# Hard-max attention on one core: last four tiles compared whole in fp32, first flag segment as words, key units of the second batch three tiles later

## The chip, the cores and the metric

One core of one Trainium2 chip runs the kernel. The metric is the device time of one execution in microseconds (us), the median of several runs. Every run also has a span, from the first to the last instruction in its trace, about 2 us shorter than the time. Unless said otherwise, times inside a run are us from the start of that span.

A **ratio** below is the mean time of one kernel's fast runs over that of the kernel before in the same rounds, so it is not quite the ratio of the medians that are quoted. Its 95% interval stands in brackets.

## The reference, cut to what matters

```python
B, Sq, Sk, D = 4, 4096, 4096, 128          # float32
logits = np.matmul(q, k.transpose(0, 2, 1))
best = np.argmax(logits, axis=-1)
return v[b_idx, best, :].astype(np.float32)
```

For each query the kernel must find the key with the largest dot product and copy that key's value row.

## The kernel before

There are 128 query tiles of 128 queries, 32 per batch. For each tile TensorE forms scores, ScalarE (ACT) and VectorE (DVE) fold groups of four keys into one packed word, and a MAX8 keeps the best eight groups. GpSimd (POOL) then **gathers** the keys of the best group (kg), VectorE forms fp16 dot products of three key differences and picks the winner, GpSimd gathers the value rows (vr), and SyncE (SP) stores them. Every gather is one GpSimd transfer of 128 rows.

Queries for which the screen is too close to call are **flagged**. They are compacted in two segments (tiles 0 to 63 during the run, tiles 64 to 127 at the end), their keys (FK) and query (FQ) are gathered in fp32 and compared exactly, the winner's value row (FV) is gathered, and a last GpSimd transfer **scatters** these rows over the output. A fallback for too many flagged rows lies behind a branch that is skipped here.

The first segment fetched the record of a flagged query (FR) before it could fetch its keys:

```python
def flag_segment(t0, t1, ready, stored):
    ...                                      # one-hot product gives tile and row: tp, rw, row, rr
    get(FR, rec, rr, P * T)                  # gather of the record
    get(FQ, q_flat, row, P * T)
    yield "until", lambda: not fast, 3
    ...                                      # bo, gi, gb from FR on VectorE
    for r in range(3):
        get(FK[:, r, :], k_flat, gb[:, r:r + 1], B * Sk)
    yield "until", lambda: not fast, 3
    win = yield from exact(FK, FQ, gb, 3, f"f{t0}")      # 12 fp32 dots on VectorE
    get(FV, v_flat, win, B * Sk)
    ...
```

The end of the kernel, where late(n) issues value gathers that are due:

```python
def flags_last(t0, t1, ready, fill, late):
    ...
    late(LATE)
    get(FK[:, 0, :], k_flat, gb[:, 0:1], B * Sk)
    get(FQ, q_flat, row, P * T)
    for r in (1, 2):
        get(FK[:, r, :], k_flat, gb[:, r:r + 1], B * Sk)
    yield                                    # whole tiles are compared here
    ...
    late(1 << 20)                            # the rest of the value gathers, then their stores
    ...
    win = whole(ex)
    all_rows(hi)                             # the skipped fallback: every engine jumps
    get(FV, v_flat, win, B * Sk)
    nc.gpsimd.indirect_dma_start(out=out_flat, out_offset=IOA(ap=rowk, axis=0), in_=FV, in_offset=None, ...)   # the scatter
```

The last two tiles are compared whole: all four keys of the best group are gathered in fp32 (xk), dotted, and picked. Key units (unit_k) prepare the next batch's keys, one ACT copy each:

```python
for b in range(1, B):
    x = b * NQT
    units += [(x - 1, x - NQT + (6 + 3 * i // 2 if b == 1 else 1 + 2 * i), unit_k, b, i) for i in range(16)]
```

## Time and profile before

| | kernel before |
|---|---|
| time, median of 3 | 438.59 us (438.47 to 438.96) |
| VectorE, ScalarE, GpSimd busy | 93%, 87%, 70% |
| last gather that waits for VectorE | 397.23 us |
| last value gather, scatter | 426.44, 432.35 us |

The page's second part shows, for 40 equal slices of the span, each engine's busy share in tenths:

```profile
DVE  2788999999999999999999999999999999999961
ACT  4999999999999999999999888999999988985010
POOL 8423456777767786777778776777767677777773
```

VectorE stays at 9 nearly to the end; GpSimd shows 7, but a gather is recorded with 1.0 us and followed by 0.3 in which GpSimd is not counted busy, so a 7 to 8 is a full GpSimd. The chain of what ended last goes on behind the two steps that the prediction shows. Columns are start, length, and what:

```profile
431.57 0.56 issue
432.12 1.25 POOLq L927
```

From the end of the scatter's last wait (431.57), 0.56 pass until GpSimd's sequencer goes on behind the scatter. The scatter itself is recorded 0.23 later, at 432.35, so **0.79 after its last wait**.

### The profile page before, as it was taken

What the parts mean: (1) busy time and instruction counts of PE and PEld (TensorE: products, weight loads), DVE (VectorE), ACT (ScalarE), POOL (GpSimd) and SP (SyncE); (2) the same over time, 40 slices, a digit from 0 to 9 for tenths busy, and PEclk for the clock granted to TensorE, in tenths of its full rate; (3) what the DMA queues carried; (4) which work ended last, traced back from release to release, by engine and by line L of the source; (5) the groups of instructions that cost most, each with busy time, mean ns of one, the idle gap of its engine ahead of it and who ended that gap; (6) DMA issues with size and microseconds to landing.
All of it is one profiled execution on the core that took longest, in us unless ns stands there. A gap on an engine that the chain in (4) does not pass through costs nothing.

```text
span 436.5 us, 6165 instructions
## 1 busy us (share of the span) xinstructions
PE 377.1 (86%) x1830; PEld 167.7 (38%) x1830; DVE 406.6 (93%) x722; ACT 378.2 (87%) x446; POOL 304.3 (70%) x335
## 2 busy tenths in 40 slices
PE   7999999999999999999999888989889988885010
PEld 4444444444444444444444433433333333332000
DVE  2788999999999999999999999999999999999961
ACT  4999999999999999999999888999999988985010
POOL 8423456777767786777778776777767677777773
PEclk9999999999999999999999999999999999999555
DMA  7943999473326999663336985452423232333441
GB/s 127 204 108 72 158 141 144 103 134 81 108 55 133 174 166 189 127 113 100 92 95 138 172 148 116 93 143 76 119 76 92 82 85 81 93 95 99 116 131 52
DMA packets 52868, 50.54 MB, mean 116 GB/s; under 512 B 34136, under 2 KB 40890, under 8 KB 52832
## 3 DMA queue, kind: packets, MB, share of 16 engines
q0 software_dynamic: 19072, 33.87, 39.7%
q1 hardware_dynamic: 33760, 16.26, 15.8%
q8 instruction: 14, 0.23, 0.2%
q14 instruction: 22, 0.18, 0.2%
HBM read 40.05 MB, written 14.55 MB: 125 GB/s over the span
## 4 chain that ended last, share of the span: by engine, by line
ACT 37%; issue 23%; DVE 16%; PE 9%; POOL 8%; DMA 6%; POOLq 0%; ACTq 0%; DVEq 0%; SPq 0%
ACT A L245 32%; DVE TOP L275 6%; ACT E L258 5%; DVE W L271 5%; POOL vr L353 4%; PE psn L228 3%; POOL kg L293 3%; PE pd L228 3%; PE psn L255 3%; DMA vr<-in_v_dram,win 2%; DMA natk<-in_k_dram 2%; DVE prod L311 1%; DVE p L316 1%; DMA vr<-in_v_dram,win_w 1%; DMA kg<-k,cand 1%
## 5 line engine op out<-in xcount | busy, mean ns | idle before, releaser
L245 ACT ACTIVATE A<-pd 128x1024 f16<-128x1024 f32 x253 | 257.0, 1043 | 10.8 <-PE pd L228 10.3
L293 POOL DMA_INDIRECT kg<-k,cand x126 | 124.5, 988 | 79.8 <-DVE cand L287 48.8
L271 DVE SCALAR_TENSOR_TENSOR W<-psn,E 128x1024 int16<-128x1024 f32 x128 | 166.4, 1300 | 6.8 <-PE psn L255 4.1
L228 PE MATMUL psn<-kT,qT 128*128 128x512 f16 x512 | 151.9, 378 | 16.2 <-ACT A L245 7.5
L228 PE MATMUL pd<-kT,qT 128*128 128x512 f16 x506 | 150.4, 379 | 6.6 <-ACT A L245 6.3
L275 DVE MAX8 TOP<-W 128x8 f32<-128x1024 f32 x128 | 156.0, 1219 | 0.0
L228 PEld LDWEIGHTS <-qT 128*128 128x128 f16 x1018 | 97.2, 97 | 153.0 <-issue 62.9
L353 POOL DMA_INDIRECT vr<-in_v_dram,win x126 | 125.9, 1000 | 39.5 <-issue 35.3
L255 PE MATMUL psn<-A,identh 128*128 128x512 f16 x512 | 152.0, 378 | 0.0
L258 ACT ACTIVATE E<-psn 128x1024 int16<-128x1024 f32 x128 | 132.3, 1033 | 4.6 <-PE psn L255 4.1
L255 PEld LDWEIGHTS <-identh 128*128 128x128 f16 x512 | 49.6, 97 | 60.8
L311 DVE TENSOR_TENSOR prod<-kg,natq 128x768 f16<-128x768 f16 x63 | 34.4, 546 | 0.2 <-DMA kg<-k,cand 0.2
L208 ACT ACTIVATE kT<-uk 128x256 f16<-128x256 f32 x48 | 20.4, 426 | 0.8 <-PE uk L205 0.8
L316 DVE TENSOR_TENSOR p<-prod 128x768 f16<-128x768 f16 (+1 forms) x34 | 17.7, 520 | 0.2
L321 DVE TENSOR_REDUCE D<-p 128x12 f32<-128x384 f16 (+1 forms) x34 | 17.2, 506 | 0.1
L204 PE MATMUL uk<-identh,natk 128*128 128x128 f16 x96 | 15.8, 218 | 0.0
L512 ACT ACTIVATE far_e<-iota_h,posn_e 128x128 f16<-128x128 f16 x2 | 0.8, 393 | 14.7 <-DVE posn_e L504 14.7
L495 PE MATMUL fp_e<-n_e,tri 128*128 128x1 f32 x2 | 0.6, 348 | 13.9 <-DVE n_e L493 13.9
L205 PEld LDWEIGHTS <-natk 128*128 128x128 f16 x96 | 9.3, 97 | 7.0 <-issue 4.5
L66 POOL DMA_DIRECT2D natk<-in_k_dram x19 | 11.3, 601 | 0.8 <-POOLq L916 0.8
L204 PEld LDWEIGHTS <-natk 128*128 128x128 f16 x96 | 9.4, 98 | 5.6
L319 DVE TENSOR_TENSOR p<-p 128x384 f16<-128x384 f16 (+1 forms) x34 | 11.3, 331 | 0.1
(158 smaller groups left out, 153.4 us busy)
## 6 DMA issues: line engine op xcount, KB each, us to landing
out_dram<-vr SPq DMA_DIRECT2D x31, 256.0 KB, 2.2
natq<-in_q_dram POOLq DMA_DIRECT2D x12, 256.0 KB, 5.3
natk<-in_k_dram POOLq DMA_DIRECT2D x10, 256.0 KB, 5.7
k<-kd SPq DMA_DIRECT2D x18, 128.0 KB, 3.4
k<-natk POOLq DMA_DIRECT2D x6, 384.0 KB
kg<-k,cand POOLq DMA_INDIRECT x126, 2.7
vr<-in_v_dram,win POOLq DMA_INDIRECT x126, 2.7
natk<-in_k_dram POOLq DMA_DIRECT2D x8, 128.0 KB, 6.5
```

What stands on the lines that cost most here:

```text
L204: nc.tensor.matmul(out=o, lhsT=natk[b % 2][:, h, 4 * m + x, :], rhs=identh, start=True, stop=False)
L208: nc.scalar.activation(out=kT[b % 2][:, c:c + 256], in_=ps, func=AF.Copy)
L228: nc.tensor.matmul(out=ps[:, n * 512:(n + 1) * 512], lhsT=qT[b % 2][:, qt * P:(qt + 1) * P], rhs=kT[b % 2][:, u * 1024 + n * 512:u * 1024 ...
L245: nc.scalar.activation(out=A, in_=ps, func=AF.Abs)
L255: nc.tensor.matmul(out=ps[:, n * 512:(n + 1) * 512], lhsT=identh, rhs=A[:, n * 512:(n + 1) * 512], start=False, stop=True)
L258: nc.scalar.activation(out=E, in_=ps, func=AF.Relu, scale=QSCALE)
L271: nc.vector.scalar_tensor_tensor(out=W_t[t % NW].bitcast(I16)[:, 1::2], in0=ps, scalar=QSCALE, in1=E, op0=OP.mult, op1=OP.max)
L275: nc.vector.max(out=TOP[:, t, :], in_=W_t[t % NW].bitcast(FP32))
L293: near_q.append(lambda j=j: nc.gpsimd.indirect_dma_start(out=kg[:, j].rearrange("p f d -> p (f d)"), out_offset=None, in_=k16[t0 // NQT], ...
L311: nc.vector.tensor_tensor(out=prod[:, i:i + h], in0=kg[:, i:i + h], in1=natq[b % 2][:, x + i - b * NQT:x + i + h - b * NQT, :].unsqueeze(2 ...
L316: nc.vector.tensor_tensor(out=p1, in0=prod[:, :, :, 0:64], in1=prod[:, :, :, 64:128], op=OP.add)
L353: late_q.append(lambda j=j: nc.gpsimd.indirect_dma_start(out=vr[:, j, :], out_offset=None, in_=v_flat, in_offset=IOA(ap=win[:, i + j:i + j ...
```

## The change

The intent was to bring the flag work of the end forward (four whole tiles behind the flag gathers, and no pick for them ahead), to save the gather FR by carrying the group words through the one-hot product, and to fill ScalarE's early tiles more evenly. Its core, cut:

```diff
-LATE = 4
+LATE = 2
+WHOLE = 4
@@ flag_segment
+        low_words(t0, S)                      # words of the three best groups
+        EC = ...; nc.vector.tensor_tensor(out=EC, in0=CG, in1=F..., op=OP.mult)
+        nc.vector.max(out=e8[:, r], in_=EC[:, r])         # r = 0..3
+        for i, x in enumerate((F, F4)):       # counts, on ScalarE now
+            nc.scalar.activation(out=junk, in_=x, func=AF.Copy, accum_out=n3[:, i:i + 1])
...
-            nc.tensor.matmul(out=ps2[:, 0:2], lhsT=OH[:, s, :], rhs=rec2[:, s, :], ...)
+            nc.tensor.matmul(out=ps2[:, 0:6], lhsT=OH[:, s, :], rhs=rec6[:, s, :], ...)
+        gb, row = places(t0, ps2)
-        get(FR, rec, rr, P * T)
         get(FQ, q_flat, row, P * T)
-        yield "until", lambda: not fast, 3
-        (bo, gi, gb from FR)
@@ pick_whole
-        put_values(len(chunks) - 1, 0, 2, win, ...)
+        for i in range(0, WHOLE, 2):
+            put_values(len(chunks) - 1, i, i + 2, win, ...)
@@ tiles per chunk
-    cuts = ... + [T - 2, T]
+    cuts = ... + [T - 6, T - 4, T]
@@ key units
-        (6 + 3 * i // 2 if b == 1 else 1 + 2 * i)
+        (9 + 3 * i // 2 if b == 1 else 1 + 2 * i)
@@ end of the program
-    drain one pick; last_picks inside flags_last; dots_whole(0); dots_whole(1)
+    drain(left("dots")); drain(left("pick")); late_now(2)
+    for i in range(WHOLE):
+        dots_whole(i)
```

Below, the three parts are called the **early shift**, the **words** and the **whole tiles**.

## The prediction

> **What bounds the kernel now.** I read the windows table by stage first, then the timelines of ScalarE (ACT) and VectorE (DVE) side by side, and last the chain that ended last with the GpSimd (POOL) timeline of the tail. Times are us from the span's start. Tiles are the 128 query tiles; a tile costs ACT two A (L245) and one E (L258), and DVE one fold W (L271), one MAX8 (L275) and a share of the fp16 dot products.
>
> ```profile
> 20.00:50.00 30.00, 28.82 (x148) 13.22 (x146) 26.37 (x27) 30.00 (x38) 11.64 (x13) 1.00 0.59 109
> 50.00:100.00 50.00, 48.68 (x247) 22.23 (x246) 49.66 (x71) 50.00 (x63) 31.19 (x33) 1.00 0.81 133
> 250.00:300.00 50.00, 45.79 (x225) 20.24 (x224) 49.90 (x88) 46.68 (x56) 37.33 (x38) 1.00 0.56 119
> 410.00:437.00 27.00, 1.95 (x10) 1.52 (x10) 13.43 (x90) 1.31 (x4) 15.56 (x15) 0.50 0.37 106
> ```
>
> Columns after the length: PE, PEld, DVE, ACT, POOL busy. From 20 to 50 ACT is full (30.00 of 30) and DVE has 3.6 us free. From 50 to about 225 both are full. From there to 397 only DVE is (49.90 of 50 against ACT's 46.68). After 410 nobody is full: this stage is a chain.
>
> The early stage, ACT and then DVE:
>
> ```profile
> 28.32 1.02 ACT L258 ACTIVATE E<-psn 128x1024 int16<-128x1024 f32 x1
> 30.14 0.39 ACT L208 ACTIVATE kT<-uk 128x256 f16<-128x256 f32 x1
> 101.46 1.12 ACT L258 ACTIVATE E<-psn 128x1024 int16<-128x1024 f32 x1
> ```
>
> ```profile
> 29.68 1.31 DVE L271 SCALAR_TENSOR_TENSOR W<-psn,E 128x1024 int16<-128x1024 f32 x1 [0.75 <-PE psn L255]
> 103.65 1.29 DVE L271 SCALAR_TENSOR_TENSOR W<-psn,E 128x1024 int16<-128x1024 f32 x1
> ```
>
> The lag from the start of a tile's E to the start of its fold is 1.36 where DVE waits (29.68 - 28.32), and I find 1.35 to 1.36 as the usual floor of waiting folds once key units run. It is 103.65 - 101.46 = 2.19 at tile 30, with no wait: there DVE is behind by its own work. The kT copy of a key unit (L208) costs ACT some 0.35 (two tiles with one take 3.08 and 3.05, those without 2.71).
>
> The tail, by POOL:
>
> ```profile
> 397.23 0.96 POOL L293 DMA_INDIRECT kg<-k,cand  x1 [0.47 <-DVE cand L287]
> 410.26 1.37 POOL L353 DMA_INDIRECT vr<-in_v_dram,win  x1 [0.30 <-issue]
> 418.51 1.01 POOL L528 DMA_INDIRECT FK<-in_k_dram,gb_e  x1 [0.30 <-DVE XD L585]
> 426.44 1.02 POOL L353 DMA_INDIRECT vr<-in_v_dram,win_w  x1 [0.30 <-issue]
> 428.30 1.00 POOL L528 DMA_INDIRECT FV<-in_v_dram,xw_fe  x1 [0.84 <-DVE xw_fe L623]
> 432.35 1.02 POOL L557 DMA_INDIRECT out_dram<-FV,rowk_e  x1 [3.05 <-DMA out_dram<-vr]
> ```
>
> and by the chain of what released what:
>
> ```profile
> 426.44 2.75 DMA vr<-in_v_dram,win_w
> 429.27 2.09 DMA out_dram<-vr
> ```
>
> The gather at 397.23 is the last one that had to wait for DVE. Behind it POOL issues 22 gathers, up to the one at 426.44, with 0.3 between each two: 29.21 / 22 = 1.33 each, and no wait. The last of them (values of the last tiles) lands, its store lands at 431.36, and only then may the scatter of the flagged rows go. The other branch, flag keys FK to winner to FV (428.30), is ready some 0.4 before the store (428.30 + 2.7 = 431.0, an estimate from the 2.7 that the page gives as the median landing of such gathers). So the end is set by the **number of POOL gathers behind 397.23**, and DVE's flag work is close behind but not on the path.
>
> **What the Trainium skill says.** "VectorE: DVE Perf Modes", in its section on the TRN2 errata, gives a two-tensor fp32 operation (N + 151)/0.96 ns; the flag product EC_e of 256 elements should be 424 ns and the trace has 0.43 us, the word build CG of 192 should be 357 and takes 0.50 us (one operand is strided 16-bit words), so I use the trace. "DMA: Bandwidth & Descriptors", section "Anatomy of one DMA", puts the fixed part of a GpSimd-issued DMA at about 2.0 us; here a gather takes 2.7 to land, and the 1.3 per gather that paces POOL is a cost of issuing, which that page calls small: the trace disagrees. "SBUF — State Buffer", section "SBUF: two separate sides", says that a VectorE instruction in a two-port mode or a GpSimd operation holds the shared port alone, and that descriptors wait for it; the gather at 410.26 took 1.37 instead of 1.00 while DVE ran a 128x768 fp16 product, which fits, though no run shows the cause. "Perfetto Trace Analysis", section "Identifying the Most-Contended Engine", goes by occupancy: that names DVE (93%), right for the middle and wrong for the tail.
>
> **The change, part by part.**
>
> *Second batch's key units three tiles later.* Nothing is added; 16 units run in iterations 9 to 31 instead of 6 to 28. Two units (0.35 each) leave the tiles before iteration 9, two come to iterations 30 and 31. ACT has no idle time from 20 to 141, so at tile 31 it is where it was. DVE is not: it waits in tiles 5 to 12, so it follows ACT and is 2 x 0.35 = 0.70 earlier from tile 9 on. At tiles 29 to 32 ACT gives the 0.70 back and the lag shrinks. It was 2.10, 2.19, 2.17, 1.83: at tile 32 it would be 1.13, under the floor of 1.36, so DVE waits 0.23 and keeps 0.70 - 0.23 = **0.47**. Later the smallest lag before tile 72 is 1.91 (tile 48); 1.44 remains, so nothing more is lost, and from 225 on DVE is the bound. Gain 0.47.
>
> *First segment as words.* It lies at tiles 73 to 105, where DVE is the bound, so I count the distance from start to start that each operation takes on DVE. Removed: product with codes 0.13, two sums 0.25, two copies from PSUM 0.13, one cast 0.06, the arithmetic from tp to row 0.07 + 0.05 + 0.11 + 0.05 + 0.06 + 0.18 + 0.08, rr 0.13, bo/gi/gb 0.27: 1.57. Added, priced from the same operations in the last segment: words 0.41, product 0.38, three MAX8 0.38, two record writes 0.24, gb/rs/row 0.37: 1.78. Net **+0.2** on DVE. ACT gets five small activations, some 0.3 each (1.5), in a stretch where it idles 3.3 of 50. POOL loses the gather FR (1.31), but the gather behind it, at 269.73, waits 1.35 for DVE anyway: worth 0. The segment's results come earlier, which nobody waits for.
>
> *Last four tiles whole.* On DVE the dots and pick of tiles 124 and 125 go (410.20 to 412.73: 2.5), one pick of a split chunk comes before the last MAX8 (0.9), so the flag work starts 1.6 earlier; one more one-hot on DVE instead of the second ACT pair brings 0.4. The gather indices gb are there at about 414.9 instead of 417.0. Eight more fp32 dots (8 x 0.215 = 1.7) come after that, before the keys land. On POOL I compared the instruction orders: two kg become two xk, and from the last gather waiting for DVE to the last value gather there are **22 steps before and after**, of the same kinds. FK moves one place ahead (two early value gathers instead of four), one value gather more follows it. FK could start at 416.8, the winner be ready at about 426.1 instead of 427.9, FV go straight behind the last value gather (427.8). But the last value gather stays at 426.4, its store at 431.4, the scatter at 432.3. What is left: the 1.37 gather may lose 0.37 as its neighbour is gone, and other gathers may meet the moved one-hots; I count -0.2.
>
> Sum: -0.47 + 0.2 - 0.2 = about -0.5; 438.6 - 0.5 = **438.1 us**.
>
> **Rivals.** (1) *The tail is DVE's*: if the flag chain sets the end, the 2.0 by which gb comes earlier arrives whole and the time is about 436.3. For it: FV waited 0.84 for the winner at 428.30. Against: the scatter waits for a store that hangs on POOL's queue, with FV landed. (2) *The longer DVE tail becomes the bound*: eight more dots and a 16-element pick put the counts and the flag winner later than the POOL queue. Worked through: dots end at 418.6, pick at 419.6, counts at 422.1, FK dots at 425.2, winner at 426.1, all ahead of POOL; it would have to be 2 off to cost 0.5 (438.9). (3) *The first segment hurts*: the new ACT operations and their wait for PE stall the A/E loop, and the ACT-PE pace falls into the 3.05 per tile that it shows from tile 97 on, against 2.9; over 10 tiles that is 1.5 (439.5). Against: the lag there is 3.3 to 3.9, so ACT is well ahead, and PSUM is emptied sooner by ACT than by the queued DVE. (4) *The early shift is worth nothing*, as ACT is full to 141: 438.6. Against: the lags.
>
> **Range and chances.** Terms: -0.47 (0 to -0.7), +0.2 (-0.4 to +0.8), -0.2 (-1.2 to +0.3), and 0.2 between runs. Together 437.1 to 438.9. 2% is 8.8 us, which no rival reaches: faster 0.01, within 2% 0.985, slower 0.005.
>
> **What would show it.** Right: lag of tile 32 near 1.4 and folds of tiles 40 to 70 about 0.5 earlier; segment operations on DVE summing to 0.2 more; the last gather that waits for DVE about 0.3 earlier (396.9); 22 gathers behind it at 1.31 to 1.33; FV within 0.4 of the end of the last value gather; the scatter still waiting for the store. Wrong: a value gather that waits for its winner, idle time on DVE in tiles 73 to 100, or the scatter released by FV.

## The result, and the profile after

The changed kernel takes **440.04 us** (439.97 to 440.70, 4 runs) against 438.53 of the kernel before in the same rounds: ratio 1.0036 [1.0019, 1.0053]. It is correct, slightly slower, and outside the predicted range of 437.1 to 438.9.

The windows table of the changed kernel, with the columns as in the prediction:

```profile
20.00:50.00 30.00, 29.13 (x142) 13.02 (x141) 26.97 (x27) 30.00 (x37) 11.68 (x13) 1.00 0.60 109
410.00:437.00 27.00, 2.04 (x10) 1.55 (x10) 14.03 (x101) 0.71 (x2) 15.68 (x16) 0.50 0.38 107
```

ScalarE is full from 20 to 50 as before; in the tail VectorE runs 101 instructions for 90. ScalarE's E of tile 30 and VectorE's fold of it, each from its engine's timeline:

```profile
101.94 1.02 ACT L257 ACTIVATE E<-psn 128x1024 int16<-128x1024 f32 x1
103.42 1.29 DVE L270 SCALAR_TENSOR_TENSOR W<-psn,E 128x1024 int16<-128x1024 f32 x1
```

The lag is 1.48, where it was 2.19: the early shift does what the prediction said. GpSimd's timeline in the tail:

```profile
397.59 0.95 POOL L292 DMA_INDIRECT kg<-k,cand  x1 [0.30 <-DVE cand L286]
426.62 1.00 POOL L352 DMA_INDIRECT vr<-in_v_dram,win_w  x1 [0.30 <-issue]
427.93 1.00 POOL L504 DMA_INDIRECT FV<-in_v_dram,xw_fe  x1 [0.30 <-issue]
433.96 1.02 POOL L533 DMA_INDIRECT out_dram<-FV,rowk_e  x1 [5.04 <-issue]
```

From the gather at 397.59 to the last value gather there are 22 steps in 29.03 (before: 29.21), and FV follows straight behind, both as predicted. But the gather at 397.59 has no wait for VectorE left (0.30 is the usual gap; it was 0.47 with the wait), and the scatter comes 1.6 later than before. The chain of what ended last shows where:

```profile
426.62 2.30 DMA vr<-in_v_dram,win_w
428.92 2.76 issue
...
431.90 1.83 issue
433.73 1.25 POOLq L904
```

Here the last wait of the scatter ends at 431.90. Then come 1.83 us of "issue", in which the engine waits for nothing that the profile shows, where the kernel before has 0.56. The scatter starts **2.06 after its last wait instead of 0.79**. Its inputs are there: FV had landed at 430.63 and the last store at 431.61, by the trace's semaphore records.

### The profile page after: what moved, and what is told of

It reads as the page before. It is cut to its first block, busy times and chain, and to the rows that moved or that the text cites. A ratio compares the mean times of both kernels' runs of the same rounds, so it can differ in the third digit from the quotient of the medians.

```text
span 438.3 us, 6171 instructions
## 1 busy us (share of the span) xinstructions
PE 378.0 (86%) x1832; PEld 168.2 (38%) x1832; DVE 407.1 (93%) x727; ACT 377.8 (86%) x451; POOL 304.0 (69%) x333
## 4 chain that ended last, share of the span: by engine, by line
ACT 37%; DVE 25%; issue 18%; PE 15%; DMA 4%; POOL 1%; POOLq 0%; ACTq 0%; DVEq 0%
ACT A L244 30%; DVE TOP L274 9%; DVE W L270 7%; ACT E L257 6%; PE psn L227 6%; PE psn L254 5%; PE pd L227 4%; DMA natk<-in_k_dram 2%; DMA FK<-in_k_dram,gb 2%; DVE prod L310 1%; DVE p L315 1%; DVE D L320 1%; DVE p L318 1%; DMA vr<-in_v_dram,win_w 1%; DVE xp_f L588 0%
## 5 line engine op out<-in xcount | busy, mean ns | idle before, releaser
L292 POOL DMA_INDIRECT kg<-k,cand x124 | 123.2, 994 | 80.0 <-DVE cand L286 49.3
L352 POOL DMA_INDIRECT vr<-in_v_dram,win x124 | 123.9, 999 | 38.9 <-issue 35.0
```

What stands on the lines that cost most here:

```text
L292: near_q.append(lambda j=j: nc.gpsimd.indirect_dma_start(out=kg[:, j].rearrange("p f d -> p (f d)"), out_offset=None, in_=k16[t0 // NQT], ...
L352: late_q.append(lambda j=j: nc.gpsimd.indirect_dma_start(out=vr[:, j, :], out_offset=None, in_=v_flat, in_offset=IOA(ap=win[:, i + j:i + j ...
```

## The experiments

Eighteen runs were made (c_only twice). The table has what their traces, and those of the two kernels, say of the scatter: how many GpSimd transfers the program executes ahead of it, and how long after its last wait it starts.

| run | transfers ahead | scatter after its last wait, us |
|---|---|---|
| kernel before | 308 | 0.79 |
| changed kernel | 307 | 2.06 |
| no_whole4 | 307 | 2.06 |
| one_store | 307 | 2.06 |
| pad8 | 307 | 2.05 |
| post4_after | 307 | 2.06 |
| fill_after | 307 | 2.07 |
| c_only, c_only_b, post4_before, a_c | 308 | 0.79 |
| twice_fq, plus1, a_c_jump, bc_plus1 | 308 | 0.78 to 0.79 |
| plus1_jump, plus1_jump_late | 308 | 0.78 to 0.79 |
| plus1_before | 309 | 0.79 |
| plus8 | 315 | 0.78 |
| drop4 | 303 | 0.79 |

### First call: each part undone, and two guesses at the late scatter

They were run on another chip.

c_only is the kernel before with one edit:

```diff
-        (6 + 3 * i // 2 if b == 1 else 1 + 2 * i)
+        (9 + 3 * i // 2 if b == 1 else 1 + 2 * i)
```

> The kernel before with the key units of the second batch three tiles later, and nothing else. Prediction's working: 0.47 us less, so about 438.1 against 438.6 (ratio 0.9989), the folds of tiles 40 to 70 about 0.45 earlier, and the scatter still about 1.0 us after the last store has landed. Rival (the shift is worth nothing, as ScalarE is full to 141 us): ratio 1.000. Rival (whatever held up the scatter of the changed kernel comes from the shift): the scatter 2.3 us after the landing.

Measured: scatter 0.79 after its last wait, so the shift does not bring the late scatter. The ratio, 0.9978 [0.9863, 1.0093], says nothing. It was run again below.

no_whole4 is the changed kernel with the tail, chunks and constants of the kernel before:

```diff
-WHOLE = 4
+WHOLE = 2
-LATE = 2
+LATE = 4
-    cuts = ... + [T - 6, T - 4, T]
+    cuts = ... + [T - 2, T]
     (flags_last and the end of the program as before)
```

> The changed kernel with one of its three parts undone: two whole tiles at the end instead of four, with the tail of the kernel before. If the late scatter (2.35 us after the last store has landed, against 0.99 before) belongs to the whole tiles, it is back at about 1.0 and the time is about 438.3 (shift -0.5, words +0.2). If the late scatter comes from the place that the GpSimd instructions have in their stream (the words take away one gather), it may stay at 2.3 and the time at about 439.6. If the words cost more than worked out, the last gather that waits for VectorE is later than 397.2 and the time is above 438.6 though the scatter comes 1.0 after the landing.

Measured: 2.06. The late scatter is there **without the whole tiles**; it comes with the words. Times unusable.

one_store is the changed kernel with one store for the last four tiles:

```diff
-        for i in range(0, WHOLE, 2):
-            put_values(len(chunks) - 1, i, i + 2, win, rows[:, NQT - WHOLE + i:NQT - WHOLE + i + 2])
+        put_values(len(chunks) - 1, 0, WHOLE, win, rows[:, NQT - WHOLE:NQT])
```

> The changed kernel with the rows of the last four tiles in one store instead of two. The scatter then waits for one semaphore fewer, as in the kernel before. If the extra store and its wait hold up the scatter: scatter 1.0 after the landing, time about 438.9 (the larger store may land 0.2 later). If the place in the stream or the idle time of GpSimd holds it up: still 2 us or more, about 440.0 to 440.4.

Measured: 2.06. The extra store and its wait are not the cause.

pad8 is the changed kernel with eight small instructions on GpSimd at tile 60:

```diff
+        if it == 60:
+            pad = cp.tile([1, 1], FP32, tag="pad")
+            for _ in range(8):
+                nc.gpsimd.memset(pad, 0.0)
```

> The changed kernel with eight tiny GpSimd memsets added at tile 60, where GpSimd has free time: all later GpSimd instructions stand eight places further in their stream. If a stall of GpSimd's sequencer at a fixed place of the stream holds up the scatter, it now falls before the waits of the scatter and is hidden: scatter 1.0 after the landing, about 438.8. If the extra store, the idle time before the scatter, or anything else in the tail does it: no change, scatter 2.3 after the landing, 440.0.

Measured: 2.05. Moving all later instructions by eight places changes nothing. What is common to the four changed kernels is that they issue one GpSimd transfer fewer than the kernel before: the gather FR.

### Second call: the jump, the idle time, or the count

post4_after and post4_before add, right behind the scatter,

```diff
+        pad = cp.tile([P, 1], FP32, tag="pad")
+        for _ in range(4):
+            nc.gpsimd.memset(pad, 0.0)
```

> The changed kernel with four tiny GpSimd memsets behind the scatter, so that the jump to the end of the program no longer follows the scatter directly. Theory P (GpSimd's sequencer stalls at the jump behind the scatter and holds the scatter back with it): the scatter starts 0.3 to 0.8 after the last wait has ended instead of 2.06, the time falls by 1.3 to 1.8. Theory Q (the scatter is held up by where it stands among the GpSimd transfers, one fewer since the first segment's gather is gone): still 2.06 after the last wait. Theory R (idle time of GpSimd ahead of it): still 2.06.

> The kernel before with the same four memsets behind the scatter. Theory P: the scatter starts 0.3 after the last wait instead of 0.79, time 0.5 less. Theories Q and R: 0.79 as it was, or, if moving the end of the program by four places brings a stall, 2.06.

Measured: 440.14 (ratio 1.0039 [1.0022, 1.0056]) and 439.10 (1.0011 [0.9994, 1.0028]). The end of the chain in post4_after:

```profile
431.52 2.06 issue
433.59 1.02 POOL out_dram L533
```

The 2.06 stand directly ahead of the scatter, with four instructions between it and the jump: theory P falls. The kernel before keeps its 0.79 with its end moved by four places.

fill_after gives GpSimd work between FV and the scatter (the four memsets take 2.28 us):

```diff
         get(FV, v_flat, win, B * Sk)
+        pad = cp.tile([P, 512], FP32, tag="pad")
+        for _ in range(4):
+            nc.gpsimd.memset(pad, 0.0)
         nc.gpsimd.indirect_dma_start(out=out_flat, ...)
```

> The changed kernel with four 128x512 memsets on GpSimd between the last value gather of the flagged rows and the scatter, while GpSimd waits for the last store. Theory R (idle time): the scatter follows the last wait in 0.8 or less. Theory P: 2.06 as before, unless the four places by which the end moves matter. Theory Q: 2.06.

Measured: 2.07, one time of 440.81. GpSimd still idles 3.39 us ahead of the scatter there, but the other traces settle it: one_store idles 2.51 and stalls, plus8 (below) idles 4.83 and does not. Theory R (idle time) falls.

twice_fq issues the query gather of the first segment twice, so the count is again 308:

```diff
         get(FQ, q_flat, row, P * T)
+        get(FQ, q_flat, row, P * T)
```

> The changed kernel with the query gather of the first segment issued twice, so that the number of GpSimd transfers is that of the kernel before again. Theory Q: the scatter follows the last wait in 0.79 again. Theory P: 2.06, unless the places by which the end moves matter. Theory R: 2.06.

Measured: 439.26 (one time), and the chain ends so:

```profile
432.24 0.55 issue
432.79 1.25 POOLq L905
```

0.55 again for 1.83, and 0.79 to the scatter. Theory Q holds so far: **the count of transfers ahead** decides.

### Third call: the count by itself

plus1 and plus8 add to the changed kernel, and plus1_before to the kernel before, gathers that nobody uses (n = 1, 8, 1):

```diff
+        if it == 43:
+            zrow = cp.tile([P, 1], U32, tag="zrow")
+            nc.gpsimd.memset(zrow, 0)
+            zbuf = cp.tile([P, P], FP32, tag="zbuf")
+        if 44 <= it < 44 + n:
+            nc.gpsimd.indirect_dma_start(out=zbuf, out_offset=None, in_=q_flat, in_offset=IOA(ap=zrow, axis=0), ...)
```

> The changed kernel with one small GpSimd gather into a scratch buffer added at tile 44, far from the tail and where GpSimd has free time. Theory Q (the stall of the scatter hangs on how many GpSimd transfers were issued ahead of it, 307 now and 308 in the kernel before): the scatter follows its last wait in 0.79 instead of 2.06, and the time falls by 1.28 to about 438.8. Rival (what mended it in the run with the query gather issued twice was the changed tail, not the count): 2.06, about 440.1.

> The same with eight small gathers, at tiles 44 to 51. The eight semaphores of GpSimd transfers are used in turn, so each transfer behind has the semaphore that it has in the changed kernel. If the stall hangs on the semaphore in turn: 2.06 from the last wait to the scatter. If it hangs on the place in a longer cycle, such as a queue of descriptors, or on there being exactly 307 transfers ahead: 0.79.

> The kernel before with one small gather added at tile 44: 309 transfers ahead of the scatter. If only the place 307 stalls: 0.79 from the last wait to the scatter, time as before. If every second place stalls: 2.06, some 1.3 longer.

Measured: plus1 439.35 (1.0021 [1.0006, 1.0035]), scatter at 0.78; its chain ends so:

```profile
432.44 0.55 issue
432.99 1.25 POOLq L911
```

plus8 452.54 (one time; eight gathers in eight tiles were too many for GpSimd's free time there, so only its scatter is used: 0.78). plus1_before 438.30 (one time), 0.79. Eight more transfers give the scatter the same semaphore as in the changed kernel, and it does not stall, so it is not the semaphore. In the counts tried (303, 307, 308, 309, 315) **only 307 stalls**, in all six traces that have it and in none of the other fourteen. The 1.28 us (2.06 - 0.78) are settled as to when they come. What happens in them no trace shows.

The traces answer three more rivals. It is not the number of GpSimd instructions ahead of the scatter: no_whole4 and drop4 both have 474, one_store and bc_plus1 476, pad8 and plus1_before 483, and of each pair only the first stalls. It is not a fetch of instructions: in five of the six stalls no DMA packet of any kind starts between the last wait and the scatter. And it is not the 308th transfer as such: in the thirteen traces with more than 308 another one has that place (FV in eleven, a value gather in plus1_before, the query gather in plus8), and it starts 0.10 after its last wait or 0.30 to 0.31 after the gather before it. What is shown is a scatter that comes late as the 308th transfer. As it is the last one in every kernel, its place and the total of 308 cannot be told apart.

The stall was worth less in time than its length: plus1 is 0.7 below the changed kernel (1.0021 against 1.0036), not 1.28. The two ratios are each good to about 0.65 us, so this may be noise; in the one trace of each, the last value gather of plus1 lands 0.34 later after its start (3.47 against 3.13).

a_c is the changed kernel with the first segment of the kernel before (early shift and whole tiles, no words):

```diff
-    (flag_segment with low_words, rec_rest, places)
+    (flag_segment as in the kernel before, with FR)
```

> The changed kernel with the first segment as in the kernel before: whole tiles and early shift without the words. 308 transfers ahead of the scatter, as in the kernel before. Theory Q: 0.79 from the last wait to the scatter; time by the prediction's terms 438.5 - 0.47 - 0.2 = 437.9, a version that beats both. Rival (the stall comes with the whole tiles): 2.06 and about 439.2.

Measured: 438.94, ratio 1.0005 [0.9991, 1.0019]; scatter at 0.79. Not the 437.9 of the prediction's terms: the late scatter is gone, and still nothing is gained.

To see what the queue does, I set each start against the start of tile 0's E, which varies by half a us from run to run (14.27 to 14.75). VectorE's fold of a tile, and the last value gather:

| run | tile 32 | tile 105 | tile 121 | tile 122 | tile 125 | last value gather |
|---|---|---|---|---|---|---|
| before | 94.94 | 318.09 | 368.58 | 372.98 | 382.60 | 412.18 |
| plus1_before | 94.94 | 318.09 | 368.57 | 372.73 | 382.36 | 411.89 |
| c_only_b | 94.44 | 317.71 | 368.23 | 372.61 | 382.24 | 411.71 |
| a_c | 94.45 | 317.75 | 368.24 | 372.49 | 382.11 | 411.61 |
| a_c_jump | 94.45 | 317.76 | 368.24 | 372.42 | 382.03 | 411.62 |
| bc_plus1 | 94.45 | 317.71 | 368.09 | 372.81 | 382.43 | 412.00 |
| after | 94.45 | 317.67 | 368.11 | 372.83 | 382.46 | 411.99 |
| plus1 | 94.44 | 317.69 | 368.09 | 372.70 | 382.37 | 412.09 |
| twice_fq | 94.44 | 317.69 | 368.25 | 372.64 | 382.27 | 412.75 |
| drop4 | 94.45 | 317.69 | 368.11 | 372.27 | 381.89 | 411.49 |
| plus1_jump | 94.44 | 318.17 | 368.37 | 372.99 | 382.66 | 412.26 |
| plus1_jump_late | 94.45 | 318.10 | 368.02 | 372.74 | 382.37 | 411.86 |

With words, in after, plus1 and bc_plus1, the step from tile 121 to 122 is 4.61 to 4.72; without them it is 4.16 to 4.40. Something holds VectorE up at tile 122. It does not come with the words in every case: twice_fq has them too, and its step is 4.38.

### Fourth call: where the rest goes

c_only_b is c_only again.

> The kernel before with the early shift alone, again, as the first run fell on a chip that ran at 534. Prediction's term: ratio 0.9989 (438.1 against 438.5). Rival (the gain is lost in tiles 121 to 125, where VectorE waits for key gathers that a full GpSimd issues late): folds 0.45 earlier at tile 105, against the start of tile 0, but within 0.1 of the kernel before at tile 125, and a ratio of 1.000.

Measured: 438.35 against 438.69, ratio **0.9988 [0.9977, 1.0000]**, by the prediction's term (0.9989). The fold of tile 105 is 0.38 earlier, that of tile 125 0.36 or 0.12, depending on which run of the kernel before one takes: both theories of the expectation stay near, but the time speaks for the term. It is the best ratio of all, though its interval ends at 1.

bc_plus1 is no_whole4 (words and early shift) with the one unused gather of plus1.

> Words and early shift with two whole tiles, and one scratch gather at tile 44, so that 308 transfers are ahead of the scatter. Prediction's terms: 0.79 from the last wait to the scatter and 438.5 - 0.47 + 0.2 = 438.2. If the words cost more than worked out: about 439, with the last gather that waits for VectorE later than 397.2 (start of tile 0 at 14.3).

Measured: 438.56, ratio 1.0004 [0.9989, 1.0019], scatter at 0.78. Against c_only_b the words cost 0.0016, some 0.7 us (worked out from the two ratios, each good to about 0.65 us), not 0.2.

drop4 leaves out four value gathers and their store, a wrong result:

```diff
         m = min(4, n - i)
+        if c == 11 and i == 0:
+            return
```

> The changed kernel without four value gathers and their store (tiles 88 to 91; a wrong result on purpose): GpSimd has 5.2 us less to do from about 305 us on. If a full GpSimd is what costs VectorE the gain in tiles 121 to 125: the fold of tile 125 comes 0.3 to 0.45 earlier against the start of tile 0 (382.0 instead of 382.45), with no wait for key gathers over 0.1 there. If not: 382.4. 303 transfers are ahead of the scatter: 0.79 from its last wait, if only 307 stalls.

Measured: fold of tile 125 at 381.89, 0.57 earlier than in the changed kernel. GpSimd, which in the changed kernel has no gap from 309 to 391, waits for VectorE again, and VectorE no longer waits for it. First GpSimd, then VectorE, in drop4:

```profile
383.02 0.94 POOL L292 DMA_INDIRECT kg<-k,cand  x1 [1.64 <-DVE cand L286]
```

```profile
384.13 0.54 DVE L310 TENSOR_TENSOR prod<-kg,natq 128x768 f16<-128x768 f16 x1
```

So **less work on GpSimd** takes the wait at tile 122 away. That a full GpSimd is what costs the fold is not shown: twice_fq and plus1_jump_late, below, are against it. The single time, 442.20, is longer for another reason: the drain behind the scatter lasted 7.17 us there against 3.25 in the kernel before. That stays unexplained.

The stretch in the changed kernel, first VectorE, then GpSimd:

```profile
380.03 0.55 DVE L310 TENSOR_TENSOR prod<-kg,natq 128x768 f16<-128x768 f16 x1
381.63 0.54 DVE L310 TENSOR_TENSOR prod<-kg,natq 128x768 f16<-128x768 f16 x1
384.74 0.56 DVE L310 TENSOR_TENSOR prod<-kg,natq 128x768 f16<-128x768 f16 x1 [0.45 <-DMA kg<-k,cand]
```

```profile
380.12 1.33 POOL L352 DMA_INDIRECT vr<-in_v_dram,win  x1 [0.30 <-issue]
381.76 1.23 POOL L292 DMA_INDIRECT kg<-k,cand  x1 [0.31 <-issue]
```

And the same place in c_only_b, GpSimd alone:

```profile
380.86 0.95 POOL L293 DMA_INDIRECT kg<-k,cand  x1 [0.31 <-issue]
382.12 1.00 POOL L353 DMA_INDIRECT vr<-in_v_dram,win  x1 [0.30 <-issue]
```

In the changed kernel two gathers start inside an fp16 product and take 1.33 and 1.23 instead of 1.0 and 0.95. The key gather that the product at 384.74 needs is the one at 381.76; in c_only_b the same one starts at 380.86, and against the start of tile 0 that is 0.78 earlier. Some 0.5 of this is there before the stretch (from about 343 on the key gathers start 0.5 later), 0.3 comes with it, and VectorE waits 0.45.

This overlap tells the traces apart better than the words or a full GpSimd do. Fifteen traces at full pace can be compared (plus8 is shifted). In the seven with a step of 4.61 to 4.72 (the changed kernel, post4_after, fill_after, plus1, bc_plus1, plus1_jump, plus1_jump_late) the two gathers take 1.13 to 1.33 and 1.23. In the eight with 4.16 to 4.41, twice_fq and drop4 among them, the gathers in their place take 1.00 to 1.01 and 0.94 to 0.95. Near 358 GpSimd waits for VectorE both in twice_fq (1.18, no overlap behind it) and in plus1_jump_late (1.24, overlap behind it), so it is full in neither, and the long step goes with the overlap. This was read from the traces afterwards; no run moves these gathers alone. In twice_fq they are:

```profile
380.79 0.94 POOL L292 DMA_INDIRECT kg<-k,cand  x1 [0.30 <-issue]
382.04 1.00 POOL L352 DMA_INDIRECT vr<-in_v_dram,win  x1 [0.30 <-issue]
```

Of the value and key gathers of the kernel before, none of the 166 that start during a fold or a MAX8 takes over 1.10; of the 37 that start during a product (prod) or during the sums behind it that read it (p<-prod), 12 do. The lengths fit what the Trainium skill says in "SBUF — State Buffer", section "SBUF: two separate sides": a GpSimd operation and a VectorE instruction that uses the shared port exclude each other. The section names two such kinds, instructions in a two-port mode and those with two inputs from SBUF, the latter only against a GpSimd operation that reads SBUF. A product of kg and natq would be of the second kind, not of the first, which the prediction named. No run here isolates that port.

a_c_jump is a_c with three additions on VectorE, about 2 us, between the flag winner and VectorE's jump over the fallback:

```diff
         win = whole(ex)
+        pad = cp.tile([P, 512], FP32, tag="pad")
+        for _ in range(3):
+            nc.vector.tensor_tensor(out=pad, in0=FK[:, 0, :], in1=FK[:, 1, :], op=OP.add)
         all_rows(hi)
```

> Whole tiles and early shift with the old first segment, and three 128x512 fp32 additions on VectorE between the winner of the flagged rows and VectorE's jump over the fallback, so that the jump comes some 2 us later. Theory J (the 8 KB instruction fetch 1.1 behind that jump delays one straggling part of the last value gather): the fetch comes after the gather's landing, the gather lands within 2.9 of its start instead of 3.5, and the time is 0.5 less than without, about 438.2. Rival (the straggler is chance): landing up to 3.5 and 438.9 as before.

Measured: 438.32, ratio 0.9997 [0.9984, 1.0010]. The last value gather landed 2.67 after its start instead of 3.50. The background is a second finding. The page's list of DMA queues has one for instructions:

```profile
q14 instruction: 22, 0.18, 0.1%
```

Each of its large packets is 8 KB. In the 16 traces at full pace, such a packet starts 1.7 to 2.6 us after the start of the last value gather in nine; in seven of these nine the last of the gather's 16 parts lands 0.51 to 1.04 after the one before it. In the seven traces without such a packet the last part follows within 0.24 (in one of them, plus1_before, a packet starts just outside, at 1.67). The Trainium skill says in "DMA: Bandwidth & Descriptors", section "Queues, rings and completion order", that a DMA engine goes round between queues by whole packets, which would let such a fetch hold up a part. The trace agrees as far as it goes. In a_c_jump the fetch (3.31 after the start) misses the gather, but it meets the **store** instead: that took 2.07 to land, against 1.79 in a_c.

### Fifth call: all three together

plus1_jump is plus1 with the three additions of a_c_jump. plus1_jump_late holds the first segment's exact comparison back as well:

```diff
-        yield "until", lambda: not fast, 3
+        yield "until", lambda: not fast, 7
         win = yield from exact(FK, FQ, gb, 3, f"f{t0}")
```

The reason for the last: with the words the 12 exact dots come some 14 us earlier on VectorE (the last at 303.28, before at 317.50), and GpSimd waits for VectorE in one piece near 309 and has no gap after it.

> The changed kernel with the scratch gather at tile 44 (308 transfers ahead of the scatter) and the three additions on VectorE ahead of its last jump. If the fetch beside the last value gather is what was left of the excess: that gather lands within 2.9 of its start (3.47 with the scratch gather alone) and the time is 0.5 below that run, about 438.8, ratio 1.0007. If not: 439.3, ratio 1.0020. The fold of tile 125 stays at 382.4 after the start of tile 0.

> The same with the first segment's exact comparison held back four tiles, to where it stood in the kernel before. If the 2.9 us for which GpSimd waits at 309, and its full queue behind it, are what cost the gain in tiles 121 to 125: no wait over 1.5 on GpSimd near 309, the fold of tile 125 at 382.1 after the start of tile 0 as in the versions without words, and the time 0.3 to 0.4 less than plus1_jump, about 438.4: level with or just under the kernel before. If the words cost by something else: 382.4 and no gain.

GpSimd's longest wait in that stretch, first in plus1_jump:

```profile
308.99 0.95 POOL L292 DMA_INDIRECT kg<-k,cand  x1 [3.14 <-DVE cand L286]
```

and the wait that stands in its place in plus1_jump_late:

```profile
306.78 0.94 POOL L292 DMA_INDIRECT kg<-k,cand  x1 [1.17 <-DVE cand L286]
```

Measured: plus1_jump 439.01, ratio 1.0013 [0.9997, 1.0028]; its last value gather landed in 2.68 (plus1: 3.47), its last store in 2.14 (plus1: 1.78). In both pairs (a_c and a_c_jump, plus1 and plus1_jump) the later jump takes 0.0008 off the ratio, 0.35 us, less than the 0.5 expected and within the intervals: the landing is shown, the gain in time is not.

plus1_jump_late took 438.76, ratio 1.0012 [0.9997, 1.0027]. The long wait is gone. Against plus1_jump the fold of tile 125 is 0.29 earlier and the last value gather 0.40, as the theory has it; but the step from tile 121 to 122 is still 4.72, tile 125 stands at 382.37 and not at 382.1, and the time does not move. Both runs are also 0.4 late at tile 105 already, where plus1 has the same program as plus1_jump and stood at 317.69, so a single trace is not good to a few tenths there. **Inconclusive**: whether the earlier exact comparison is what makes the words dear stays open.

## Why the prediction was wrong

**The step that failed** is in the whole tiles: "But the last value gather stays at 426.4, its store at 431.4, the scatter at 432.3." Gather and store came as said (426.62, landed 431.61). The scatter was taken to follow the store as before, and came at 433.96. One transfer had left the program in tile 83 (the gather FR, at 266.11 in the kernel before; the prediction called its loss "worth 0"), which put 307 transfers ahead of the scatter, and with 307 it stalls 1.28 us longer. That the count decides is shown by twice_fq and plus1, which add one transfer in two different places, and by every other run of the table.

**The sizes that were off.** The rest of the miss is 440.04 - 438.1 - 1.28 = 0.66 us. It agrees with the queue: against the start of tile 0 the last value gather stands at 411.87 in three runs of the kernel before and its variants (412.18, 411.53, 411.89) and at 411.93 to 412.08 after (411.99; post4_after 411.93, fill_after 412.08), where the prediction's -0.5 would have put it at 411.4. By parts:

- *Early shift, -0.47*: right. Up to tile 30 VectorE is 0.60 earlier (predicted 0.70), tile 32's lag is 1.35 (predicted near 1.4), its fold 0.50 earlier; alone the shift gives 0.9988, 0.5 us.
- *Words, +0.2*: the count of VectorE work was not the trouble: from tile 72 to 106 the fold loses 0.08 to c_only_b, at tile 125 0.13 to 0.22 (plus1, bc_plus1, after; single traces, and the kernel before's own differ by 0.24 there). What the term left out is GpSimd. In the changed kernel GpSimd is full from 309 to 391, the last gather that had waited 0.47 for VectorE waits no longer, and VectorE waits for a key gather at tile 122; the last value gather is 0.3 later than in c_only_b. drop4 shows that less work on GpSimd takes the wait away, and in all seven traces with the long step two gathers overlap products. Why they fall together there, and why GpSimd is full with one transfer less to do, stays open: twice_fq, with the words, shows neither, and holding the exact comparison back gave no clear answer.
- *Whole tiles, -0.2*: the working of the tail was right nearly to the tenth (gb at 414.8, predicted 414.9; FV at 427.93, predicted 427.8; 22 steps), and the queue ends 0.10 earlier in a_c than in c_only_b. In time it is no gain: 1.0005 against 0.9988. VectorE's jump now comes beside the last value gather's landing, but that this costs the time is not shown: in c_only_b's trace another such packet meets that gather, and it lands later still (3.86 against a_c's 3.50). The difference is within the intervals and stays open.

These times by parts (-0.5, +0.7, +0.7, and 1.28 for the stall) add up to 2.2 us against 1.6 measured. Each is good to about 0.65, so I do not lean on their sum. The trace's 1.28 is the firm part; the queue's 0.6 is good to some 0.3, as the three values of the kernel before show.

**The rivals.** Rival 1 (the tail is VectorE's) is refuted: FV came 0.4 earlier and nothing followed. Rival 2 (the longer VectorE tail binds) is refuted: no value gather waited for a winner. Rival 3 named the words as the danger, but by a stall of the A/E loop; that loop caught up by tile 110, and what was lost later was lost to a wait for GpSimd. Rival 4 (shift worth nothing) is refuted by the folds, nearly in time too.

**Of the signs listed for "wrong"** none appeared: no value gather waiting for its winner, no idle VectorE in tiles 73 to 100, no scatter released by FV. Two of the signs for "right" failed: the last gather that waits for VectorE was to come at 396.9, and that gather comes at 397.59 without a wait, and the scatter no longer starts when its wait for the store ends. The main error sat in an interval that I had read off once, 0.99 from landing to scatter, and carried over without asking what sets it.

No version beats both kernels beyond doubt. The early shift alone is the best, 438.35 against 438.69 of the kernel before in the same rounds, with an interval that reaches 1.0000.

## What to carry to other kernels

An interval on the critical path that the profile calls "issue" has a cause too: before carrying it over, ask what the change does to the count and order of what that engine has issued, and when it moves, add one unused transfer far away to see whether the count sets it. When two engines are both nearly full, a change on one can show up as a wait of the other tens of tiles later; set the starts of the same tile in both traces against the start of the first tile and look for the step where they part. Three gains of a few tenths each are below what the ends of gathers, stores and instruction fetches do by chance of timing, so test such parts one by one.

## What the Trainium skill lacked or had wrong

- "DMA: Bandwidth & Descriptors" tells of the descriptor rings of GpSimd's transfers, but not that a transfer can start late by its place in their sequence: with 307 transfers ahead the scatter, the last one, starts 2.05 to 2.07 us after its last wait (six traces), with 303, 308, 309 or 315 ahead 0.78 to 0.79 (fourteen).
- The same page, in section "Anatomy of one DMA", calls the time to generate a GpSimd transfer's descriptors small; here 22 gathers take 29.03 us one behind the other, 1.32 each, and this sets the tail.
- "Advanced Engine Details and Errata", section "Control Flow Timing", gives about 108 ns for a compare-and-branch. The trace has 0.07 for VectorE's jump over the fallback.
- No page gives what a fetch of instructions can cost a transfer that is landing. An 8 KB packet started 1.56 behind VectorE's jump in the changed kernel and 1.1 behind it in the kernel before, and in seven of nine traces where such a packet met the last gather, its last part came 0.51 to 1.04 late.
- No page says how much the landing of one and the same gather varies: 2.58 to 3.87 us for the last value gather in the sixteen traces at full pace.
